# Quartered input tiles, q projections inside the norm loop, and projection blocks cut into pieces between the steps of an mLSTM scan

## The chip, the cores and the metric

One Trainium2 chip, all 8 cores of it, each with one sequence of the batch; there is no traffic between cores. The time is that of the slowest core, in device microseconds (us). Most executions agree within 0.3% (the fast ones of the kernel before lie between 3200.28 and 3208.29 us). Some fall into a second, slower state, in which the cores of one die, sometimes of both, run at a lower granted TensorE clock (0.80 to 0.96 in place of 0.97 to 0.99; the granted clock is the share of full speed that the profile records).

## The reference, cut to what matters

A decoder layer: RMS norm, one input projection, two groups of heads beside each other (dilated attention and an mLSTM), an output projection, then a gated MLP with a convolution. The change is in the norm, the mLSTM's projections and the mLSTM itself.

```python
h = _rmsnorm(x, norm_mix_g[layer]).astype(x.dtype)         # x: (8, 2048, 2048)
proj = h @ w_in[layer]
aq, ak, av, mq, mk, mv, mo, mi, mf = jnp.split(proj, IN_SPLITS, axis=-1)
...
qk = jax.nn.silu(_causal_dwconv(jnp.concatenate([mq, mk], axis=-1), ...))   # 4 taps
hm = _mlstm(mq_c, mk_c, mv, mi + b_igate, mf + b_fgate)    # 4 heads of 128, chunks of 128
hm = hm * jax.nn.sigmoid(mo)
hm = _rmsnorm(hm, mlstm_norm_g)
```

`_mlstm` goes through 16 chunks of 128 tokens in order. Each chunk computes its scores, an output from scores and carried state, and a new state for the next chunk.

## The kernel before: the parts that matter

Names used below: TensorE (PE in the profile), VectorE (DVE), ScalarE (ACT). Each engine works through its own list in program order (in the kernel before, the last matmul of a state update began at 427.07 us, but VectorE's part of the update only at 429.17, behind two operations that stand ahead of it in VectorE's list); semaphores hold an instruction until its inputs are there (VectorE stood idle until 0.10 us after ScalarE's Exp, L359, in seven tiles of eight). TensorE writes its sums into the program's eight PSUM buffers, called banks below; a bank is written again when ScalarE or VectorE has read it (TensorE waits 32.7 us in all for VectorE's reading of one in the scan of the kernel before; ScalarE's copy out of a bank is called an eviction below). "Gates" in the first stage are the mLSTM's input and forget gates; the output gate comes in the scan.

First stage: for every tile of 256 tokens, ScalarE squares all of x, TensorE sums the squares over the 2048 features with a matrix of ones, ScalarE makes 1/sqrt of it (Ln, Exp), VectorE normalises in 16 instructions, and TensorE projects v (two blocks of 16 matmuls) and the gates. The q and k projections come only after all eight tiles.

```python
def norm_a(tt):
    K.op(act, ... activation(out=sq, in_=x_t, func=AF.Square), [B_x], [B_sq])          # whole tile
    K.mm([... matmul(pb[:, 0:TA], ones, sq[:, kc, :]) for kc in range(KC)], [B_sq, B_one], [B_pb])
    ...                                                    # Ln, Exp, 16 x scalar_tensor_tensor
    if tt + 3 < NTA:
        xin(tt + 3)                                        # one 2 MB transfer into the freed tile
norm_a(0)
norm_a(1)
for tt in range(NTA):
    for tb in (2 * tt, 2 * tt + 1):
        mv_proj(tb)
    if tt + 2 < NTA:
        norm_a(tt + 2)
```

The scan: 64 dense projection blocks (16 for the output gate, 48 for the attention's v, 16 matmuls of 512 columns each) are poured between the steps of the chunks to keep TensorE busy. `next(work)` emits one whole block.

```python
for c in range(-1, NCH):
    sc_pre(c + 1)          # TensorE: scores, transposes of k, decay sums; ScalarE: Exp of the decay sums
    next(work)             # one block
    sc_out(c)              # TensorE: numerator and denominator of the output
    sc_fin(c - 1)          # TensorE: RMS sum of the chunk before; ScalarE Ln, Exp; VectorE; store
    sc_pre2(c + 1)         # VectorE: decay mask on the scores; ScalarE: scaled k
    sc_out2(c)             # ScalarE, VectorE: divide, output gate; ScalarE: Square for the RMS sum
    next(work)
    next(work)             # two blocks
    sc_upd(c, 0); sc_upd(c, 1)   # TensorE, then VectorE: new state
    if c % 2:
        next(work)         # one more after odd chunks
```

(Conditions for the first and last chunks are cut.) Scores and half of the state update share one PSUM bank, so the scores of a chunk wait until VectorE has read the update before (13 waits, 32.7 us). The decay sums and the RMS sum share another, so the RMS sum waits until ScalarE's decay Exp has read the decay sums (one wait of 0.3 us in this kernel).

The softmax here doesn't subtract the row's maximum and nothing guards it: scores larger than these inputs give would overflow.

## Time and profile before

| | us |
|---|---|
| median of 15 runs | 3206.04 |
| profiled run, slowest core (core 2) | 3205.0 |
| its first scores of the scan / first decay sums | 278.8 / 283.8 |
| its attention starts | 609.8 |
| from there to the end | 2595.2 |

Two of the waits of the first 284 us (engine and line that waited, for whom; us in total, times, longest). The line numbers are those of the kernel before:

```profile
DVE mem L361 <- ACT mem L359: 77.3, 8, 27.4
PE ps L356 <- ACT mem L355: 65.8, 8, 24.4
```

Eight waits each, one for every tile: TensorE (L356, the ones-matmuls) stands behind the Square (L355), and VectorE's normalising (L361) behind the Exp (L359). The longest of each, 24.4 and 27.4 us, is that of the first tile, while x is still landing. Together with the tile of the timeline that the prediction shows, this is a relay: one engine runs while the others stand.

### The profile page before, as it was taken

What the parts mean: (1) busy time and instruction counts of PE and PEld (TensorE: products, weight loads), DVE (VectorE), ACT (ScalarE), POOL (GpSimd) and SP (SyncE); (2) the same over time, 40 slices, a digit from 0 to 9 for tenths busy, and PEclk for the clock granted to TensorE, in tenths of its full rate; (3) what the DMA queues carried; (4) which work ended last, traced back from release to release, by engine and by line L of the source; (5) the groups of instructions that cost most, each with busy time, mean ns of one, the idle gap of its engine ahead of it and who ended that gap; (6) DMA issues with size and microseconds to landing.
All of it is one profiled execution on the core that took longest, in us unless ns stands there. A gap on an engine that the chain in (4) does not pass through costs nothing.

```text
span 3205.0 us, 43522 instructions; the slowest of 8 cores (3171.3 to 3205.0 us)
## 1 busy us (share of the span) xinstructions
PE 2929.6 (91%) x14807; PEld 1389.2 (43%) x15100; DVE 1786.4 (56%) x2452; ACT 1184.0 (37%) x1890; POOL 197.3 (6%) x347
## 2 busy tenths in 40 slices
PE   3799888999999994999899999999999978998999
PEld 2444444444444442444344444444444433443444
DVE  2465344355555551344878777777778874334333
ACT  2345544355565551111444444444444430000000
POOL 0000000000000000000111000000001100000000
PEclk8899999999999997999999999999999989999999
DMA  9232233531332309446555343334336767779784
GB/s 213 65 49 31 42 58 58 107 59 43 64 65 37 65 11 195 164 145 153 84 101 88 66 67 66 66 63 70 66 61 106 168 144 144 152 146 236 148 150 97
DMA packets 232952, 313.65 MB, mean 98 GB/s; under 512 B 24224, under 2 KB 155296, under 8 KB 230688
## 3 DMA queue, kind: packets, MB, share of 16 engines
q0 software_dynamic: 95088, 142.76, 30.8%
q1 hardware_dynamic: 137648, 168.10, 18.0%
q8 instruction: 125, 2.05, 0.3%
q14 instruction: 91, 0.75, 0.1%
HBM read 382.23 MB, written 71.30 MB: 142 GB/s over the span
## 4 chain that ended last, share of the span: by engine, by line
PE 76%; DMA 8%; DVE 8%; issue 4%; ACT 3%; DVEq 0%; another core or an unknown queue 0%; SPq 0%; ACTq 0%
PE ps L1070 43%; PE ps L709 9%; PE ps L1000 6%; PE ps L424 3%; DMA mem<-xT 3%; PE ps L508 2%; DMA mixd<-mem 2%; DMA mem<-actd 2%; PE ps L787 1%; PE ps L727 1%; DMA actd<-mem 1%; PE ps L800 1%; PE ps L372 1%; PE ps L494 1%; DVE mem L924 1%
## 5 line engine op out<-in xcount | busy, mean ns | idle before, releaser
L1070 PE MATMUL ps<-mem 128*128 128x512 bf16 x7276 | 1615.2, 381 | 77.8 <-DVE mem L924 38.9
L1070 PEld LDWEIGHTS ps<-mem 128*128 128x128 bf16 x7424 | 726.9, 98 | 965.8 <-issue 108.3
L1125 DVE SCALAR_TENSOR_TENSOR mem<-mem,cfs 128x1024 f32<-128x1024 f32 x352 | 452.0, 1284 | 225.7 <-ACT mem L1119 184.6
L709 PE MATMUL ps<-mem 128*128 128x512 bf16 x1511 | 372.3, 379 | 4.6 <-ACT mem L513 0.9
L924 DVE TENSOR_TENSOR mem<-mem 128x1024 bf16<-128x1024 bf16 (+3 forms) x324 | 305.9, 979 | 61.7 <-DMA mem<-w_down 45.0
L1091 ACT ACTIVATE mem<-ps 128x512 f32<-128x512 f32 x264 | 156.8, 594 | 424.0 <-PE ps L1070 409.8
L1253 DVE TENSOR_TENSOR mem<-ps,mem 128x512 f32<-128x512 f32 x128 | 88.3, 691 | 304.7 <-PE ps L1070 282.8
L1000 PE MATMUL ps<-mem 128*128 128x512 bf16 x1003 | 233.9, 384 | 23.2 <-DMA mem<-mixd 22.1
L1119 ACT ACTIVATE mem<-mem,cfs 128x1024 f32<-128x1024 f32 x176 | 216.9, 1233 | 11.7 <-DVE mem L1095 7.5
L709 PEld LDWEIGHTS ps<-mem 128*128 128x128 bf16 x1536 | 148.9, 98 | 162.5 <-issue 17.5
L166 POOL DMA_DIRECT2D mem<-w_up x240 | 127.4, 533 | 1237.3 <-PE ps L1070 748.7
L790 DVE TENSOR_TENSOR mem<-mem 128x512 bf16<-128x512 bf16 x216 | 88.0, 417 | 179.7 <-ACT mem L789 179.7
L720 DVE SCALAR_TENSOR_TENSOR mem<-ps,cfs,mem 128x512 bf16<-128x512 f32 x192 | 143.3, 746 | 76.7 <-ACT mem L718 66.0
L508 PE MATMUL ps<-mem 128*128 128x512 bf16 x749 | 175.6, 389 | 1.6 <-issue 0.4
L1095 DVE TENSOR_TENSOR mem<-ps,mem 128x512 f32<-128x512 f32 x264 | 172.9, 683 | 1.3 <-PE ps L1070 1.2
L1000 PEld LDWEIGHTS ps<-mem 128*128 128x128 bf16 x1024 | 101.1, 99 | 146.1 <-issue 27.9
L789 ACT ACTIVATE mem<-ps 128x512 bf16<-128x512 f32 x216 | 126.7, 589 | 88.5 <-PE ps L787 87.0
L1012 DVE TENSOR_TENSOR mem<-ps,mem 128x512 f32<-128x512 f32 x64 | 44.3, 692 | 177.3 <-PE ps L1020 107.6
L1017 ACT ACTIVATE mem<-mem 128x512 bf16<-128x512 f32 x64 | 40.2, 629 | 239.9 <-DVE mem L1012 239.9
L508 PEld LDWEIGHTS ps<-mem 128*128 128x128 bf16 x768 | 77.0, 101 | 90.2 <-issue 8.6
L361 DVE SCALAR_TENSOR_TENSOR mem<-mem,cfs 128x256 bf16<-128x256 f32 x128 | 62.0, 484 | 90.7 <-ACT mem L359 77.3
L424 PE MATMUL ps<-mem 128*128 128x512 bf16 x501 | 111.6, 383 | 0.8 <-issue 0.2
(118 smaller groups left out, 2321.9 us busy)
## 6 DMA issues: line engine op xcount, KB each, us to landing
mem<-w_up POOLq DMA_DIRECT2D x240, 256.0 KB, 5.0
mem<-w_down POOLq DMA_DIRECT2D x60, 640.0 KB, 8.2
actd<-mem SPq DMA_DIRECT2D x88, 256.0 KB, 3.9
mem<-actd SPq DMA_DIRECT2D x16, 1280.0 KB, 17.2
mem<-xT SPq DMA_DIRECT2D x8, 2048.0 KB, 20.5
mem<-xT SPq DMA_DIRECT2D x64, 256.0 KB, 3.3
x1d<-mem SPq DMA_DIRECT2D x64, 256.0 KB, 3.7
mem<-x1d SPq DMA_DIRECT2D x64, 256.0 KB, 5.2
```

The source lines that it names most:

```text
L166: eng.e.dma_start(out=o_, in_=i_).then_inc(sb.dsem, 16)
L424: bk, B_bk = dense(5, [lambda e, b, kc=kc: e.matmul(b[:], sl[:, kc, hm * 128:(hm + 1) * 128], hT[:, kc, tsl], start=(kc == 0), stop=(kc == ...
L508: bk, B_bk = dense(3, [lambda e, b, kc=kc: e.matmul(b[:], hT[:, kc, c0:c0 + 128], sl[:, kc, :], start=(kc == 0), stop=(kc == KC - 1)) for ...
L709: ins = pe.e.matmul(bank[:], sl[:, kc, c0:c0 + 128], hT[:, kc, tsl], start=(kc == 0), stop=(kc == KC - 1))
L720: K.op(dve, lambda e: e.scalar_tensor_tensor(out=sc[nm], in0=bank[:], scalar=cf[:, gcol:gcol + 1], in1=tab[:, tsl], op0=ALU.mult, op1=ALU. ...
L924: K.op(dve, lambda e: e.tensor_tensor(out=out, in0=a, in1=b, op=op), [B_a, B_b], [B_out])
L1000: K.mm([lambda e, kc=kc: e.matmul(ps[bi][:], wo_v[jb][:, kc, (jc % 4) * 128:(jc % 4 + 1) * 128], mixT[:, T, kc, :], start=(kc == 0), stop= ...
L1070: K.mm([lambda e, l=l, r=r, s_=(first and i == 0): e.matmul(ps[bi][:], l, r, start=s_, stop=False, skip_group_check=True) for i, (l, r) in ...
L1091: K.op(act, lambda e: e.activation(out=snap[si], in_=ps[bank][:], func=AF.Copy), [B_ps[bank]], [B_snap[si]])
L1095: K.op(dve, lambda e: e.tensor_tensor(out=y, in0=ps[bank][:], in1=snap[si], op=ALU.add), [B_ps[bank], B_snap[si]], [self.B_y[gv]])
L1119: K.op(act, lambda e: e.activation(out=self.a[gv], in_=self.y[gv][:, 2:1026], func=AF.Identity, scale=self.wc(gv, 2), bias=cf[:, CF_FCB + ...
L1125: K.op(dve, lambda e, k=k: e.scalar_tensor_tensor(out=self.a[gv], in0=self.y[gv][:, k:k + 1024], scalar=self.wc(gv, k), in1=self.a[gv], op ...
```

## The change

Its intent: in the first stage, fill TensorE's pauses with q projection blocks, and square x ahead of its use; in the scan, take the dense block out from between the scores and the output, and spread the filler evenly.

```diff
@@ first stage @@
+    # x tile moved to make room: the third one lies over the space of the constants cb
     def xin(tt):
-        K.dma(sp, xs[tt % 3], xT_v[:, :, tt * TA:(tt + 1) * TA], B_xs[tt % 3], True)
+        for q in range(4):
+            K.dma(sp, xs[tt % 3][:, 4 * q:4 * q + 4, :], ..., B_xs[tt % 3][q], True)
...
-    K.dma(pool, cb[:], cbd, B_cb, True)          # now behind the q projections
+    def norm_sq(tt): ...                         # four Squares, one for each quarter
+    def norm_h(tt): ...                          # ones-matmuls by quarters, Ln, Exp, normalise
...
+    norm_sq(0); norm_h(0); norm_sq(1); norm_h(1)
+    mv_proj(0); norm_sq(2); mv_proj(1); norm_h(2)
+    for tt in range(2, NTA):
+        if tt + 1 < NTA:
+            norm_sq(tt + 1)
+        mq_proj(2 * tt - 4)
+        if tt + 1 < NTA:
+            mq_proj(2 * tt - 3)
+            norm_h(tt + 1)
+        mv_proj(tt)
+    for i in range(11, 16):
+        mq_proj(i)
...                                              # gate constants moved behind this point
@@ scan @@
+        def block(lr, reads):                    # a dense block that yields after every 4 matmuls
...
-            sc_pre(c + 1)
-        next(work)
+            sc_pre(c + 1)
+        if c < 0:
+            some(4)
...
             sc_out2(c)
-        next(work)
-        next(work)
+        some(8)                                  # 8 pieces = two blocks
+        if ok(c):
+            sc_sq(c)                             # the Square that ended sc_out2
...
             sc_upd(c, 1)
-        if c % 2:
-            next(work)
+        some(6)                                  # one and a half blocks
```

The number of matmuls is the same.

More of the change, by code (lines that the diff above doesn't have):

```diff
@@ L296, in build @@
     xs, B_xs = [], []
-    for i, o in enumerate((0, 16384, 49152)):
-        v, B = alloc(A0 + o, KC * TA, F32, "xs%d" % i)
-        xs.append(v.rearrange("p (k t) -> p k t", t=TA))
-        B_xs.append(B)
-    o = A0 + 65536
-    gt, B_gt = alloc(o, 128, F32, "gt")
-    e1, B_e1 = alloc(o + 512, 64, F32, "e1")
-    lf, B_lf = alloc(o + 768, 64, F32, "lf")
-    ib, B_ib = alloc(o + 1024, 64, F32, "ib")
-    ebias, B_eb = alloc(o + 1280, 64, F32, "ebias")
-    gt, e1, lf, ib, ebias = [a.rearrange("p (c g) -> p c g", c=16) for a in (gt, e1, lf, ib, ebias)]
-    OT = o + 1792
+    for i, o in enumerate((A0 + 16384, A0 + 49152, 160768)):
+        v = mview(o, KC * TA, F32).rearrange("p (k t) -> p k t", t=TA)
+        xs.append(v)
+        B_xs.append([K.mbuf("xs%d_%d" % (i, q), o + q * 4096, o + (q + 1) * 4096) for q in range(4)])
+    OG = A0 + 65536
+    OT = OG + 1792
     o = OT
-    sqA, B_sqA, rsA, B_rsA = [], [], [], []
+    sqA, B_sqA = [], []
     for i in range(2):
-        v, B = alloc(o, KC * TA, BF16, "sqA%d" % i)
-        sqA.append(v.rearrange("p (k t) -> p k t", t=TA))
-        B_sqA.append(B)
+        sqA.append(mview(o, KC * TA, BF16).rearrange("p (k t) -> p k t", t=TA))
+        B_sqA.append([K.mbuf("sqA%d_%d" % (i, q), o + q * 2048, o + (q + 1) * 2048) for q in range(4)])
         o += 8192
-        v, B = alloc(o, TA, F32, "rsA%d" % i)
-        rsA.append(v)
-        B_rsA.append(B)
-        o += 1024
+    rsA, B_rsA = zip(*[alloc((OG, o)[i], TA, F32, "rsA%d" % i) for i in range(2)])
+    o += 1024
     acc, B_acc, xp, B_xp = [], [], [], []
@@ L332, in build @@
     tl, B_tl = alloc(o, 32, F32, "tl")
+    assert o + 128 <= 160768
     tl = tl.rearrange("p (j w) -> p j w", w=4)
@@ L340, in xin, with by_tile @@
     def xin(tt):
-        K.dma(sp, xs[tt % 3], xT_v[:, :, tt * TA:(tt + 1) * TA], B_xs[tt % 3], True)
+        for q in range(4):
+            K.dma(sp, xs[tt % 3][:, 4 * q:4 * q + 4, :], xT_v[:, 4 * q:4 * q + 4, tt * TA:(tt + 1) * TA], B_xs[tt % 3][q], True)
+    def by_tile(b, lo, hi):
+        bl = [K.buf(b.name) for _ in range(NT)]
+        for b_ in bl:
+            K.inherit(b_, [b])
+            K.regions.append((lo, hi, b_))
+        return bl
     xin(0)
@@ L349, in build, with norm_sq, norm_h @@
     w_issue()
-    K.dma(pool, cb[:], cbd, B_cb, True)
-    def norm_a(tt):
-        x_t, B_x, sq, B_sq, r, B_r = xs[tt % 3], B_xs[tt % 3], sqA[tt % 2], B_sqA[tt % 2], rsA[tt % 2], B_rsA[tt % 2]
+    def norm_sq(tt):
+        x_t, sq = xs[tt % 3], sqA[tt % 2]
+        for q in range(4):
+            qs = slice(4 * q, 4 * q + 4)
+            K.op(act, lambda e: e.activation(out=sq[:, qs, :], in_=x_t[:, qs, :], func=AF.Square),
+                 [B_xs[tt % 3][q]], [B_sqA[tt % 2][q]])
+    def norm_h(tt):
+        x_t, sq, r, B_r = xs[tt % 3], sqA[tt % 2], rsA[tt % 2], B_rsA[tt % 2]
         pb, B_pb = ps[6 + tt % 2], B_ps[6 + tt % 2]
-        K.op(act, lambda e: e.activation(out=sq, in_=x_t, func=AF.Square), [B_x], [B_sq])
-        K.mm([lambda e, kc=kc: e.matmul(pb[:, 0:TA], ones, sq[:, kc, :], start=(kc == 0), stop=(kc == KC - 1))
-              for kc in range(KC)], [B_sq, B_one], [B_pb])
+        for q in range(4):
+            K.mm([lambda e, kc=kc: e.matmul(pb[:, 0:TA], ones, sq[:, kc, :], start=(kc == 0), stop=(kc == KC - 1))
+                  for kc in range(4 * q, 4 * q + 4)], [B_sqA[tt % 2][q], B_one], [B_pb])
         K.op(act, lambda e: e.activation(out=r, in_=pb[:, 0:TA], func=AF.Ln, scale=1.0 / D, bias=EPS), [B_pb], [B_r])
@@ L362, in norm_a @@
                 out=hT[:, kc, tt * TA:(tt + 1) * TA], in0=x_t[:, kc, :], scalar=cf[:, CF_G1 + kc:CF_G1 + kc + 1],
-                in1=r, op0=ALU.mult, op1=ALU.mult), [B_x, B_r, B_cf], [B_hT[tt]])
+                in1=r, op0=ALU.mult, op1=ALU.mult), [B_xs[tt % 3][kc // 4], B_r, B_cf], [B_hT[tt]])
         if tt + 3 < NTA:
             xin(tt + 3)
-    slot, B_slot = w_next()
-    sl = wv(slot)
-    def mv_proj(tb):
-        c0 = tb * 128
-        bk, B_bk = dense(5, [lambda e, b, kc=kc: e.matmul(b[:], hT[:, kc, c0:c0 + 128], sl[:, kc, :], start=(kc == 0),
-                                                          stop=(kc == KC - 1)) for kc in range(KC)],
-                         [B_slot, B_hT[tb // 2]])
-        K.op(act, lambda e: e.activation(out=mvt[:, tb, :], in_=bk[:], func=AF.Copy), [B_bk], [B_mv])
-        K.mm([lambda e, kc=kc: e.matmul(ps[5][:, tb * 8:(tb + 1) * 8], hT[:, kc, c0:c0 + 128], wg[:, kc, :],
-                                        start=(kc == 0), stop=(kc == KC - 1)) for kc in range(KC)],
-             [B_hT[tb // 2], B_wg], [B_ps[5]])
@@ L380, in build, with mv_proj @@
-    norm_a(0)
-    norm_a(1)
-    for tt in range(NTA):
-        for tb in (2 * tt, 2 * tt + 1):
-            mv_proj(tb)
-        if tt + 2 < NTA:
-            norm_a(tt + 2)
-    w_issue()
+    w_mv, B_wmv = w_next()
+    w_mq, B_wmq = w_next()
+    w_mv, w_mq = wv(w_mv), wv(w_mq)
+    def mv_proj(tt):
+        for tb in (2 * tt, 2 * tt + 1):
+            c0 = tb * 128
+            bk, B_bk = dense(5, [lambda e, b, kc=kc: e.matmul(b[:], hT[:, kc, c0:c0 + 128], w_mv[:, kc, :],
+                                                              start=(kc == 0), stop=(kc == KC - 1)) for kc in range(KC)],
+                             [B_wmv, B_hT[tt]])
+            K.op(act, lambda e: e.activation(out=mvt[:, tb, :], in_=bk[:], func=AF.Copy), [B_bk], [B_mv])
+            K.mm([lambda e, kc=kc: e.matmul(ps[5][:, tb * 8:(tb + 1) * 8], hT[:, kc, c0:c0 + 128], wg[:, kc, :],
+                                            start=(kc == 0), stop=(kc == KC - 1)) for kc in range(KC)],
+                 [B_hT[tt], B_wg], [B_ps[5]])
@@ new lines, in build, with conv_proj @@
+    pend_silu = []
+    def conv_proj(part, sl, B_slot, dstT, B_d, tt, hm):
+        tsl = slice(tt * TT, (tt + 1) * TT)
+        bk, B_bk = dense(5, [lambda e, b, kc=kc: e.matmul(b[:], sl[:, kc, hm * 128:(hm + 1) * 128], hT[:, kc, tsl],
+                                                          start=(kc == 0), stop=(kc == KC - 1))
+                             for kc in range(KC)], [B_slot] + hTt(tt))
+        j = part * 4 + hm
+        wc = lambda k: cf[:, CF_MCW + j * 4 + k:CF_MCW + j * 4 + k + 1]
+        xi = rot["xp"]
+        rot["xp"] += 1
+        x_, B_x, a_, B_a = xp[xi % 3], B_xp[xi % 3], acc[xi % 2], B_acc[xi % 2]
+        K.op(act, lambda e: e.activation(out=x_[:, 3:3 + TT], in_=bk[:], func=AF.Copy), [B_bk], [B_x])
+        K.op(act, lambda e: e.activation(out=a_, in_=bk[:], func=AF.Identity, scale=wc(3),
+                                         bias=cf[:, CF_MCB + j:CF_MCB + j + 1]), [B_bk, B_cf], [B_a])
+        while pend_silu:
+            pend_silu.pop(0)()
+        K.op(dve, lambda e: e.tensor_copy(out=x_[:, 0:3], in_=tl[:, j, 0:3]), [B_tl[j]], [B_x])
+        for k in (2, 1, 0):
+            K.op(dve, lambda e, k=k: e.scalar_tensor_tensor(out=a_, in0=x_[:, k:k + TT], scalar=wc(k), in1=a_,
+                                                            op0=ALU.mult, op1=ALU.add), [B_x, B_cf, B_a], [B_a])
+        K.op(dve, lambda e: e.tensor_copy(out=tl[:, j, 0:3], in_=x_[:, TT:TT + 3]), [B_x], [B_tl[j]])
+        pend_silu.append(lambda: K.op(act, lambda e: e.activation(out=dstT[:, hm, tsl], in_=a_, func=AF.Silu),
+                                      [B_a], [B_d[tt]]))
@@ new lines, in build @@
+    mqT, B_mq = alloc(A0, 4 * S, BF16, "mqT")
+    mqT = mqT.rearrange("p (h t) -> p h t", t=S)
+    B_mq = by_tile(B_mq, A0, A0 + 16384)
+    mq_proj = lambda i: conv_proj(0, w_mq, B_wmq, mqT, B_mq, i // 4, i % 4)
+    norm_sq(0)
+    norm_h(0)
+    norm_sq(1)
+    norm_h(1)
+    mv_proj(0)
+    norm_sq(2)
+    mv_proj(1)
+    norm_h(2)
+    for tt in range(2, NTA):
[6 more added lines that the diff above has]
+        mv_proj(tt)
@@ new lines, in build @@
+    w_issue()
+    for i in range(11, 16):
+        mq_proj(i)
+    w_issue()
+    while pend_silu:
+        pend_silu.pop(0)()
+    K.dma(pool, cb[:], cbd, B_cb, True)
+    gt, B_gt = alloc(OG, 128, F32, "gt")
+    e1, B_e1 = alloc(OG + 512, 64, F32, "e1")
+    lf, B_lf = alloc(OG + 768, 64, F32, "lf")
+    ib, B_ib = alloc(OG + 1024, 64, F32, "ib")
+    ebias, B_eb = alloc(OG + 1280, 64, F32, "ebias")
+    gt, e1, lf, ib, ebias = [a.rearrange("p (c g) -> p c g", c=16) for a in (gt, e1, lf, ib, ebias)]
@@ L402, in gates_2 @@
         K.op(act, lambda e: e.activation(out=ebias, in_=ib, func=AF.Exp), [B_ib], [B_eb])
-    mqT, B_mq = alloc(A0, 4 * S, BF16, "mqT")
     mkT, B_mk = alloc(A0 + 16384, 4 * S, BF16, "mkT")
     sgo, B_sgo = alloc(A0 + 49152, 4 * S, BF16, "sgo")
-    mqT, mkT, sgo = [a.rearrange("p (h t) -> p h t", t=S) for a in (mqT, mkT, sgo)]
-    def by_tile(b, lo, hi):
-        bl = [K.buf(b.name) for _ in range(NT)]
-        for b_ in bl:
-            K.inherit(b_, [b])
-            K.regions.append((lo, hi, b_))
-        return bl
@@ L415, in build @@
-    B_mq, B_mk = by_tile(B_mq, A0, A0 + 16384), by_tile(B_mk, A0 + 16384, A0 + 32768)
-    pend_silu = []
-    for part in range(2):
-        slot, B_slot = w_next()
-        sl = wv(slot)
-        dstT, B_d = (mqT, B_mq) if part == 0 else (mkT, B_mk)
-        for tt in range(NT):
-            tsl = slice(tt * TT, (tt + 1) * TT)
-            for hm in range(NHM):
-                bk, B_bk = dense(5, [lambda e, b, kc=kc: e.matmul(b[:], sl[:, kc, hm * 128:(hm + 1) * 128], hT[:, kc, tsl],
-                                                                  start=(kc == 0), stop=(kc == KC - 1))
-                                     for kc in range(KC)], [B_slot] + hTt(tt))
-                if part == 0 and tt == 0 and hm == 0:
-                    gates_2()
-                j = part * 4 + hm
-                wc = lambda k: cf[:, CF_MCW + j * 4 + k:CF_MCW + j * 4 + k + 1]
-                xi = rot["xp"]
-                rot["xp"] += 1
-                x_, B_x, a_, B_a = xp[xi % 3], B_xp[xi % 3], acc[xi % 2], B_acc[xi % 2]
-                K.op(act, lambda e: e.activation(out=x_[:, 3:3 + TT], in_=bk[:], func=AF.Copy), [B_bk], [B_x])
-                K.op(act, lambda e: e.activation(out=a_, in_=bk[:], func=AF.Identity, scale=wc(3),
-                                                 bias=cf[:, CF_MCB + j:CF_MCB + j + 1]), [B_bk, B_cf], [B_a])
-                while pend_silu:
-                    pend_silu.pop(0)()
-                K.op(dve, lambda e: e.tensor_copy(out=x_[:, 0:3], in_=tl[:, j, 0:3]), [B_tl[j]], [B_x])
-                for k in (2, 1, 0):
-                    K.op(dve, lambda e, k=k: e.scalar_tensor_tensor(out=a_, in0=x_[:, k:k + TT], scalar=wc(k), in1=a_,
-                                                                    op0=ALU.mult, op1=ALU.add), [B_x, B_cf, B_a], [B_a])
-                K.op(dve, lambda e: e.tensor_copy(out=tl[:, j, 0:3], in_=x_[:, TT:TT + 3]), [B_x], [B_tl[j]])
-                pend_silu.append(lambda d=dstT[:, hm, tsl], a_=a_, B_a=B_a, B_d=B_d[tt]: K.op(
-                    act, lambda e: e.activation(out=d, in_=a_, func=AF.Silu), [B_a], [B_d]))
-        w_issue()
@@ L447, in build @@
+    mkT, sgo = [a.rearrange("p (h t) -> p h t", t=S) for a in (mkT, sgo)]
+    B_mk = by_tile(B_mk, A0 + 16384, A0 + 32768)
+    slot, B_slot = w_next()
+    sl = wv(slot)
+    for i in range(16):
+        conv_proj(1, sl, B_slot, mkT, B_mk, i // 4, i % 4)
+        if i == 0:
+            gates_2()
+    w_issue()
     pend_silu.pop(0)()
@@ L488, in dense_work @@
     def dense_work():
+        def block(lr, reads):
+            bi = rot["mm"] % 3
+            rot["mm"] += 1
+            K.deps(pe, reads, [B_ps[bi]])
+            for kc in range(KC):
+                ins = pe.e.matmul(ps[bi][:], *lr(kc), start=(kc == 0), stop=(kc == KC - 1))
+                if kc % 4 == 3 and kc < KC - 1:
+                    yield
+            K.mark(pe.sig(ins), reads, [B_ps[bi]])
+            blk[:] = ps[bi], B_ps[bi]
+        blk = [None, None]
         slot, B_slot = w_next()
@@ L493, in dense_work @@
             for hm in range(NHM):
-                bk, B_bk = dense(3, [lambda e, b, kc=kc: e.matmul(b[:], sl[:, kc, hm * 128:(hm + 1) * 128], hT[:, kc, tsl],
-                                                                  start=(kc == 0), stop=(kc == KC - 1))
-                                     for kc in range(KC)], [B_slot] + hTt(tt))
+                yield from block(lambda kc: (sl[:, kc, hm * 128:(hm + 1) * 128], hT[:, kc, tsl]), [B_slot] + hTt(tt))
+                bk, B_bk = blk
                 K.op(act, lambda e: e.activation(out=sgt, in_=bk[:], func=AF.Exp, scale=-1.0), [B_bk], [B_sgt])
@@ L507, in dense_work @@
                 c0 = tb * 128
-                bk, B_bk = dense(3, [lambda e, b, kc=kc: e.matmul(b[:], hT[:, kc, c0:c0 + 128], sl[:, kc, :],
-                                                                  start=(kc == 0), stop=(kc == KC - 1))
-                                     for kc in range(KC)], [B_slot, B_hT[tb // 2]])
+                yield from block(lambda kc: (hT[:, kc, c0:c0 + 128], sl[:, kc, :]), [B_slot, B_hT[tb // 2]])
+                bk, B_bk = blk
                 v_, B_v = vst[rot["vs"] % 3], B_vst[rot["vs"] % 3]
@@ L571, in sc_out2, with sc_sq @@
         K.op(dve, lambda e: e.tensor_tensor(out=hg, in0=hg, in1=sgo[:, :, csl], op=ALU.mult), [B_hg, B_sgo], [B_hg])
+    def sc_sq(c):
+        hg, B_hg = hg2[c % 2], B_hg2[c % 2]
         K.op(act, lambda e: e.activation(out=sqh, in_=f4(hg), func=AF.Square), [B_hg], [B_sqh])
@@ L622, in build, with some @@
     work = dense_work()
+    def some(n):
+        for _ in range(n):
+            next(work)
     ok = lambda c: 0 <= c < NCH
@@ L642, in build @@
             sc_upd(c, 1)
-        if c % 2:
-            next(work)
-    next(work)
+        some(6)
     sc_fin(NCH - 1)
@@ L1567, in run @@
     for b in range(ncores):
-        in_maps.append({"xT": np.ascontiguousarray(inp["x"][b].T), "w_in": w_in, "w_out": w_out, "w_up": w_up,
+        in_maps.append({"xT": np.ascontiguousarray(inp["x"][b].T),
+                        "w_in": w_in, "w_out": w_out, "w_up": w_up,
                         "w_down": w_down, "cb": cbn, "cf": cfn, "cs": cs})
```

## The prediction, made before the changed kernel ran

> **What bounds the kernel now.** I read the page first, then the busy time by stage, then the timeline of the first 170 us, then the chain of waits inside the mLSTM scan. Stage limits come from where the first instruction of each line falls: norm and mLSTM v projection 0 to 163 us, q and k projections with their convolution to 284, scan to 610, then attention, output projection and ConvFFN. Busy time by stage (start and end, length; PE, weight loads, DVE, ACT, POOL; granted clock; DMA share; GB/s):
>
> ```profile
> 0.00:284.00 284.00, 208.83 (x1174) 106.18 (x1194) 144.43 (x294) 108.33 (x141) 9.61 (x14) 0.90 0.47 94
> 284.00:610.00 326.00, 285.95 (x1621) 154.26 (x1654) 123.76 (x234) 158.83 (x285) 4.91 (x5) 0.93 0.31 58
> 610.00:1238.00 628.00, 581.40 (x3672) 294.53 (x3742) 336.73 (x551) 351.75 (x600) 15.65 (x14) 0.98 0.34 62
> 1500.00:3205.00 1705.00, 1619.20 (x7294) 728.57 (x7441) 1095.29 (x1256) 522.70 (x797) 160.76 (x303) 0.99 0.57 110
> ```
>
> The change touches only the first two rows. In both, PE is idle some of the time and its clock is below full; nothing after 610 us is edited, so what those two stages lose or gain should arrive at the end unchanged. One tile of the first stage, on the timeline:
>
> ```profile
> 88.72 3.61 ACT L355 ACTIVATE mem<-mem 128x4096 bf16<-128x4096 f32 x1
> 92.47 3.32 PE L356 MATMUL ps<-mem,ones 128*128 128x256 bf16 x16 [4.02 <-ACT mem L355]
> 96.42 0.42 ACT L359 ACTIVATE mem<-mem 128x256 f32<-128x256 f32 x1
> 96.93 9.31 DVE L361 SCALAR_TENSOR_TENSOR mem<-mem,cfs 128x256 bf16<-128x256 f32 x16 [6.79 <-ACT mem L359]
> 99.48 3.61 PE L372 MATMUL ps<-mem 128*128 128x512 bf16 x16
> 104.05 3.61 ACT L355 ACTIVATE mem<-mem 128x4096 bf16<-128x4096 f32 x1
> ```
>
> Square (3.61 us) runs alone, PE waits 4.02 us for it, then sums the squares at half speed (3.32 us for 16 matmuls of 256 columns). A tile takes 15.3 us here (88.72 to 104.05), of which real projection work is about 7.7. In the scan, this is one lap of the chain of waits (start, length, what), cut:
>
> ```profile
> 413.82 0.38 PE ps L522 x4
> 415.38 3.45 PE ps L508 x16
> 420.04 0.61 ACT mem L603
> 421.46 0.70 DVE mem L606
> 427.77 0.70 DVE mem L570
> 429.17 0.49 DVE mem L592
> 431.35 0.59 PE ps L522 x4
> ```
>
> It is a loop: scores of the next chunk (L522), a dense projection block of 3.45 us (L508), the outputs, the RMS sums, ACT, then DVE's in-order list from L606 to the state update L592, which frees the score bank for the next L522. So the lap lasts 17.53 us, and the dense block in it is on the path, not filler. The waits of PE in the scan say the same:
>
> ```profile
> PE ps L522 <- DVE mem L592: 32.7, 13, 5.2
> ```
>
> [...] after the idle gaps of the norm, weight loads stand 0.43 us apart, later a block of 16 takes 3.45 us, 0.216 each. [...] the granted clock is 1.00 from 180 to 230 us with PE busy 49.74 of 50 us. [...] L592, whose matmuls ended at 427.1, waits for L571 ahead of it. [...] The trace shows 1.28 us and the Silu starting right after (176.98, 178.27), so I use 1.28. [...] while the weights stream beside them, x tiles take about 18 us each (19.2, 38.0, then 72.3 landed), with the DMA share at 1.0 until 80 us.
>
> **The change, part by part.** First, x comes in quarters, each with its own Square and its own four ones-matmuls. On tiles 0 and 1 only the last quarter remains behind the landing: 0.95 us instead of 3.62, and 0.9 instead of 3.5. x tile 1 landed at 38.0, so the first v block starts near 40.0 instead of 45.2. Saves 5.
>
> Second, Square is issued a tile ahead and mq blocks are put into the norm loop. PE work of a full iteration, at full clock: two mq blocks 6.9, ones-matmuls [...] 1.7, two v blocks with gates 7.7 (3.86 each): 16.3 us. Does another engine exceed that? DVE: normalise 9.31 plus two convolutions of 2.9 = 15.1. ACT: Square 3.8, four conv copies 2.8, two Silus 1.25, Ln and Exp 0.8, two evictions 1.2, and two table loads 2.6, because Silu and Ln/Exp now alternate: 12.5. (That is about 12 more loads, 15 us of ACT, hidden if PE is the bound.) The latency from the ones-matmuls to a finished hT is 3.1 + 9.3 = 12.4 us, against 16.3 until the v blocks want it. So 16.3 stands.
>
> The clock of this stage then reads: first v blocks 40.0; the second pair needs hT of tile 1, 50.7, and ends at 58.5; ones-matmuls of tile 2 to 60.3; the first mq block needs the second weight slot, which landed 58.5 us after its issue at 5.8, so 64.3: a new wait of 4 us; tile 3 of x lands near 70 and the iteration ends at 80.7. Four full iterations: 145.9. Last: one mq and two v blocks, 11.2: 157.1. Then five mq blocks, 17.3: 174.4. The k weights can start only when the v blocks are done, and the same load took 19.0 us before: they land at 176.5 to 177, a new wait of 2.5. Then k blocks 55.2, gate cumsum 3.7 and about 1: scan at 237 instead of 284. Saves 47 (the 5 above included). The constant load moved behind it is not wanted until the scan.
>
> Third, the scan. Taking the dense block out from between scores and outputs shortens the lap from 17.53 to 14.1 us. PE's own work per chunk is 3.5 blocks x 3.45 = 12.1, plus scores, transposes and decay sums 1.56, outputs 0.9, RMS sum 0.2, update 0.45: 15.2. PE so becomes the bound with a margin of 1 us[...]. I take 15.6 for small waits. Before, ten laps from 376.14 to 564.90 took 18.88 each: 3.28 saved on eleven laps is 36. The first four laps also carry the output gate, three ACT passes a block: ACT needs some 14 us of 15, and stands ahead of the decay Exp, so I take 17.5 against 18.5, saving 4. The last waits save 2. Sum 42. Square moved behind the dense blocks only frees ACT, which was idle 26.9 us there; PE had not waited for it.
>
> Sum: 47 + 42 = 89. 3206 - 89 = 3117 us, 2.8% less.
>
> **Rivals.** (a) The norm loop turns DVE- or ACT-bound: DVE has 15.1 of 16.3 us, and each semaphore hop costs it 0.1. For it: convolution and normalise alternate behind table loads. Against: hT has 3.9 us of slack. If an iteration takes 18.5, 2.2 x 5 = 11 us go: 3128. (b) Weights arrive too late for the compressed stage: both waits above (4 and 2.5) grow if the x quarters take more of the DMA. Against: dropping the constants from the early queue leaves more. Worth up to 12: 3129. (c) The scan stays latency-bound: the margin is 1 us, and Cbf, the decay Exp and the evictions share one ACT queue. If a lap takes 17 instead of 15.6, 15 us go: 3132. (d) The gain is given back later, at the attention start or by a lower clock. Against: attention, at 97% busy PE, is fed by the same sequence of prefetches, and the clock holds 1.00 in dense stages. If half the gain went: 3161. [...]
>
> **Range and chances.** (a), (b) and (c) are each likely in part and would add up to about 3150 only together; the upside is some 15 us. I predict 3117, with 3096 to 3145 holding it 8 times in 10. Over 2% faster means under 3142: 0.87. Within 2%: 0.12. Slower by over 2%: 0.01, since no instruction is added on the path but hidden table loads.
>
> **What would show it.** The first gate cumsum decay matmul of the scan (L527 before) should start near 237 instead of 283.8: later than 245 means (a) or (b), and the waits of PE tell which, DVE's normalise or the weight DMA. Attention should start 89 us earlier, near 521, and the time from there to the end should stay 2595. Laps of the scan should be 15 to 16 us with PE's wait for L592 gone from its list; if a wait for ACT's decay Exp or for Cbf stands there instead, it is (c). The granted clock should rise to about 0.97 in both stages. About 16 table loads should appear where 4 were. A span after attention longer than before would show (d), and my premise that the stages add up would be wrong.

The 1.28 us at 176.98 is a table load, ScalarE's ACT_TABLE_LOAD, in front of the first Silu. Of the 16 matmuls of 256 columns on that timeline (from 92.47), most start 0.213 us apart, at a granted clock of 0.50 (92.1 to 95.3 us); the last two stand 0.110 us apart.

## The result, and the profile after

| | before | after |
|---|---|---|
| median of all runs, us | 3206.04 (15 runs) | 3123.06 (11 runs) |
| ratio | | 0.9742, 95% interval 0.9733 to 0.9752 |
| first scores, mean of 8 cores | 278.1 | 241.5 |
| attention starts, mean of 8 cores | 608.7 | 531.2 |
| end, mean of 8 cores | 3187.8 | 3109.6 |
| TensorE clock, mean of the slowest core | 0.968 | 0.980 |

The ratio is the mean time of one kernel's fast runs over that of the other's fast runs of the same rounds, so it is not quite the ratio of the two medians. The change makes the kernel 2.6% faster, 83 us by the medians; 89 were predicted. By the means of the cores of the two profiled runs it is 78.

The rows by core come from one profiled run each: the time from a core's first instruction to the first one of a line. Two profiled runs of the very same kernel (the second is told below) differ by 1.6 us in the first scores, by 1.3 in the length of the scan and by 3.7 in what comes after, always as means of the cores; the cores of one run spread by 20 to 31 us in what comes after. Differences below that say nothing. So the stages read: first stage 36.6 us shorter, scan 40.9 shorter (330.6 to 289.7), the rest unchanged (2579.1 and 2578.4).

Line numbers of the two kernels, for reading what follows:

| | before | after |
|---|---|---|
| Square of x, ones-matmuls, normalise | L355, L356, L361 | L356, L363, L368 |
| v blocks; q and k blocks | L372; L424 | L381; L393 |
| gate log; gate cumsum on TensorE | L394; L397 | L453; L456 |
| scores; decay sums; decay Exp | L522; L527; L529 | L559; L564; L566 |
| dense blocks of the scan | L494, L508 | L522 |
| state update on VectorE; RMS sum | L592; L602 | L632; L642 |

Busy time by stage on the slowest core after the change (its columns as in the prediction's first fence; the stages are cut at its own first scores, attention and ConvFFN):

```profile
0.00:240.80 240.80, 199.16 (x1162) 100.63 (x1184) 138.92 (x286) 124.25 (x173) 8.45 (x13) 0.98 0.55 110
240.80:532.60 291.80, 273.73 (x1630) 146.56 (x1660) 128.01 (x243) 160.74 (x288) 6.22 (x6) 0.98 0.35 65
532.60:1118.90 586.30, 568.19 (x3570) 286.08 (x3641) 327.29 (x534) 340.44 (x581) 12.20 (x11) 1.00 0.29 54
1421.40:3121.00 1699.60, 1616.85 (x7279) 726.79 (x7425) 1093.69 (x1254) 521.88 (x796) 160.21 (x303) 0.99 0.57 109
```

The clock rose from 0.90 and 0.93 to 0.98 in both stages, and in the scan TensorE is busy 94% of the time (273.73 of 291.80) where it was 88% (285.95 of 326.00), while its busy time itself fell by 12 us: the same matmuls at a higher clock (the median of the decay sums' matmuls went from 328 to 275 ns).

One iteration of the norm loop, on the timeline after:

```profile
95.86 6.85 PE L393 MATMUL ps<-mem 128*128 128x512 bf16 x31
96.05 3.88 ACT L356 ACTIVATE mem<-mem 128x1024 bf16<-128x1024 f32 x4
...
102.55 1.91 PE L363 MATMUL ps<-mem,ones 128*128 128x256 bf16 x16
...
104.29 3.62 PE L381 MATMUL ps<-mem 128*128 128x512 bf16 x15
...
105.13 1.28 ACT L365 ACT_TABLE_LOAD   x1
...
107.42 9.32 DVE L368 SCALAR_TENSOR_TENSOR mem<-mem,cfs 128x256 bf16<-128x256 f32 x16 [0.18 <-ACT mem L366]
...
112.22 6.85 PE L393 MATMUL ps<-mem 128*128 128x512 bf16 x31
```

Read the PE lines: two q blocks, the ones-matmuls in 1.91 us, 0.109 apart (3.32 before), two v blocks, and the next q blocks at 112.22. None of these lines carries a wait in brackets. The Square of the next tile (96.05) now lies under the q blocks. The iteration takes 16.36 us and holds two more blocks than a 15.3 us tile did before.

A steady lap of the scan, in the chain of waits after, with `...` for the outputs and the state update's 0.06 us pieces:

```profile
377.02 0.22 PE ps L559 x4
...
377.46 0.95 PE ps L564 x8
...
379.30 0.32 PE ps L642
...
380.76 5.78 PE ps L522 x26
...
390.27 1.89 PE ps L522 x8
392.16 0.22 PE ps L559 x4
```

Before, this chain ran through ScalarE and VectorE; now every piece of it is PE's own. The lap is 15.14 us long (377.02 to 392.16), where 17.5 and 20.1 alternated. What TensorE still waits for in the scan:

```profile
PE ps L642 <- ACT mem L566: 10.4, 5, 3.4
PE ps L564 <- DVE mem L558: 4.4, 1, 4.4
```

The 32.7 us of waits for the state update are gone. The 4.4 us wait at the scan's start was there before. The first line is new in this size (one wait of 0.3 us before): it is the RMS sum that waits for the decay Exp, the sign that the prediction gave for its rival (c).

One more new wait stands between the stages. TensorE, and one ScalarE line, at the first k block:

```profile
176.31 3.61 PE L393 MATMUL ps<-mem 128*128 128x512 bf16 x16 [1.46 <-DMA mem<-w_in]
...
179.94 1.28 ACT L451 ACT_TABLE_LOAD   x1
182.39 5.57 PE L456 MATMUL ps<-mem,cfs 128*128 128x4 f32 x32 [2.47 <-DVE mem L453]
...
188.20 53.01 PE L393 MATMUL ps<-mem 128*128 128x512 bf16 x235 [0.24 <-issue]
```

The k weights come 1.46 us late, and the gate cumsum then waits 2.47 us for the gates' log, and runs slower after it (5.57 us; 3.63 before). The first k matmuls behind it are slow, too: their weight loads stand 0.43 us apart from 188.20 to 190.76, where 0.22 is usual.

### The profile page after: what moved, and what is told of

It is laid out like the page before. It is cut to its first block, busy times and chain, and to the rows that moved or that the text cites. A ratio compares the mean times of both kernels' runs of the same rounds, so it can differ in the third digit from the quotient of the medians.

```text
span 3121.2 us, 43707 instructions; the slowest of 8 cores (3093.6 to 3121.2 us)
## 1 busy us (share of the span) xinstructions
PE 2908.4 (93%) x14805; PEld 1376.0 (44%) x15100; DVE 1784.8 (57%) x2452; ACT 1201.4 (38%) x1926; POOL 196.9 (6%) x347
## 4 chain that ended last, share of the span: by engine, by line
PE 79%; DMA 7%; DVE 6%; issue 4%; ACT 3%; SPq 1%; DVEq 0%; another core or an unknown queue 0%; ACTq 0%; POOLq 0%; POOL 0%
PE ps L1114 44%; PE ps L753 10%; PE ps L1044 6%; PE ps L522 6%; PE ps L393 3%; DMA mixd<-mem 2%; DMA actd<-mem 2%; PE ps L831 1%; PE ps L771 1%; PE ps L381 1%; DMA mem<-actd 1%; PE ps L844 1%; PE ps L772 1%; DVE mem L1215 1%; DVE mem L968 1%
## 5 line engine op out<-in xcount | busy, mean ns | idle before, releaser
L1114 PE MATMUL ps<-mem 128*128 128x512 bf16 x7276 | 1616.4, 381 | 78.7 <-DVE mem L968 40.1
L1114 PEld LDWEIGHTS ps<-mem 128*128 128x128 bf16 x7424 | 726.7, 98 | 968.0 <-issue 111.0
L753 PE MATMUL ps<-mem 128*128 128x512 bf16 x1500 | 371.9, 379 | 4.6 <-ACT mem L550 0.9
L1044 PE MATMUL ps<-mem 128*128 128x512 bf16 x1004 | 233.9, 384 | 22.1 <-DMA mem<-mixd 21.1
L522 PE MATMUL ps<-mem 128*128 128x512 bf16 x994 | 229.6, 385 | 2.2 <-issue 0.8
L753 PEld LDWEIGHTS ps<-mem 128*128 128x128 bf16 x1536 | 148.9, 98 | 162.6 <-issue 17.6
L1044 PEld LDWEIGHTS ps<-mem 128*128 128x128 bf16 x1024 | 101.1, 99 | 145.1 <-issue 27.1
L522 PEld LDWEIGHTS ps<-mem 128*128 128x128 bf16 x1024 | 100.9, 99 | 119.3 <-issue 7.3
L393 PE MATMUL ps<-mem 128*128 128x512 bf16 x499 | 112.9, 385 | 5.4 <-DMA mem<-w_in 4.3
L1215 DVE TENSOR_TENSOR mem<-mem 128x1024 bf16<-128x1024 f32 x88 | 106.8, 1213 | 4.3 <-DMA actd<-mem 4.1
```

The source lines that it names most:

```text
L393: bk, B_bk = dense(5, [lambda e, b, kc=kc: e.matmul(b[:], sl[:, kc, hm * 128:(hm + 1) * 128], hT[:, kc, tsl], start=(kc == 0), stop=(kc == ...
L522: ins = pe.e.matmul(ps[bi][:], *lr(kc), start=(kc == 0), stop=(kc == KC - 1))
L753: ins = pe.e.matmul(bank[:], sl[:, kc, c0:c0 + 128], hT[:, kc, tsl], start=(kc == 0), stop=(kc == KC - 1))
L1044: K.mm([lambda e, kc=kc: e.matmul(ps[bi][:], wo_v[jb][:, kc, (jc % 4) * 128:(jc % 4 + 1) * 128], mixT[:, T, kc, :], start=(kc == 0), stop= ...
L1114: K.mm([lambda e, l=l, r=r, s_=(first and i == 0): e.matmul(ps[bi][:], l, r, start=s_, stop=False, skip_group_check=True) for i, (l, r) in ...
L1215: K.op(dve, lambda e: e.tensor_tensor(out=ao[i], in0=self.a[0], in1=self.a[1], op=ALU.mult), [self.B_a[0], self.B_a[1]], [B_ao[i]])
```

## The experiments

All use the changed kernel ("after") as the base, except where told. Times are of fast runs; "scan" is from the first scores to the start of attention, mean of the cores, and 289.7 us in the changed kernel.

### The two stages apart

The old scan behind the new first stage, and the new scan behind the old first stage:

```diff
 # stage only: after, with dense_work, sc_out2 and the chunk loop of the kernel before
 # scan only:  the kernel before, with dense_work, sc_out2/sc_sq and the chunk loop of after
```

> The changed first stage (norm, v, q and k projections) with the old scan. If the two parts simply add: the first scores of the scan start about 37 us earlier than before (241.5 against 278.1 us, mean of the cores), the scan lasts as long as before (331 us) and the whole comes to about 3206 - 37 = 3169 us. Rival, the gain of one part depends on the other (for instance weights for the scan that now come too late, or the clock): the scan is then longer than 335 us and the time above 3175.

> The changed scan behind the old first stage. If the parts add: scores start at 278 us as before, the scan lasts 290 us instead of 331, the whole about 3206 - 41 = 3165 us. Rival as in the run beside it: a time above 3172 or a scan above 295 us would say that part of its gain came from the first stage.

Measured: stage only 3161.1 us (only one of its four runs was fast, so there is no interval), first scores at 240.6, scan 328.0. Scan only 3157.9 to 3160.5 us, ratio 0.9859 (0.9837 to 0.9882), first scores at 278.3, scan 287.4. The kernel before took 3203 to 3206 beside them. So each part gives its gain without the other, 43 and 45 us by the means of the fast runs, and the sum of 88 is near the 83 of both; the 5 us between are about the scatter of such sums. The expectations were 8 us too high for the stage (3169) and 6 for the scan (3165).

### The dense block put back into the lap

The one part undone that the prediction calls the cause in the scan:

```diff
-        if c < 0:
-            some(4)
+        some(4)
...
-        some(6)
+        some(6 if c < 0 else 2)
```

> The changed kernel with one change undone: a whole dense block (four pieces) stands again between the scores and the outputs of every chunk, and four pieces fewer behind the state update; the split of blocks into pieces, 3.5 blocks per chunk, the moved Square and the first stage stay. Theory, the block was on the lap of waits: a lap goes from 15.1 back to about 14.1 + 3.45 = 17.5 us, PE waits for the state update of DVE again, and the whole is some 11 to 15 laps x 2.4 = 26 to 36 us longer than the changed kernel: 3149 to 3159. Rival, the gain came from spreading the filler evenly[...]: laps stay under 16 us and the time within 8 us of 3123.

Measured: 3154.5 to 3158.9 us, ratio 0.9851 (0.9829 to 0.9874), scan 321.1. That is 34 us slower than the changed kernel, and the scan accounts for 31 of them. TensorE's list of waits has its old entry back:

```profile
PE ps L559 <- DVE mem L632: 32.6, 13, 3.2
```

13 waits and 32.6 us, against 13 waits and 32.7 us in the kernel before. The fine split, the even 3.5 blocks and the moved Square were all still in this kernel. So the place of the block is worth 31 of the scan's 41 us, because the block stands on the lap's chain of waits, and the rival, that even filling brings the whole gain, falls. It does not bring the old laps back in full: over the last ten they average 18.1 us here on the slowest core, 18.9 in the kernel before and 15.9 in the changed one, and the 20.1 us laps have become 17.5 to 19.2. The other 10 us belong to the rest of the scan's edit (split, even spread, Square) together; with the block on the lap no run takes these apart.

### Whole blocks in place of pieces

```diff
-        some(6)
+        some(4 if c < 0 or c % 2 == 0 else 8)
```

> The changed kernel with whole dense blocks only: behind the state update one block after even chunks and two after odd ones, in place of one and a half each. Theory: with three blocks TensorE has only 10.35 + 3.1 = 13.5 us of work in a lap that the chain of waits holds at 14.1 or more, so half of the laps gain a wait of 0.6 to 1 us and the others none: the scan is 4 to 8 us longer (294 to 298) and the time near 3129. Rival, the split is without effect: within 2 us of the run beside it[...].

Measured, beside a repeat of the changed kernel on the same chip:

> The changed kernel unaltered, run again beside the next three on the same chip, so that differences of some us can be read: about 3123 us, first scores at 241 us, scan 290 us.

The repeat took 3123.9 to 3128.8 us (ratio 0.9754, scan 288.4), whole blocks 3122.0 to 3128.2 (ratio 0.9751, scan 288.7): no difference. My expectation was wrong in its sum, though its mechanism showed. On the slowest core six new waits for the state update came, 4.0 us together, as worked out for laps with three blocks; two waits for ScalarE's bf16 copy of the state (2.7 us) came too, but the waits for ScalarE's decay Exp fell from some 8 to 11 us per core in the repeat to 4.1 to 4.6 (3.2 of dense blocks and 1.4 of RMS sums on that core). One paid for the other. The laps say the same: the later ones alternate between 14.18 and 16.87 us, 15.5 in the mean, where the changed kernel has 15.14, but two laps of 19.1 us that it has (explained below) are gone. So an even lap is worth 0.4 us, and in the whole scan cutting blocks in half is worth nothing here.

### The moved Square

```diff
     def sc_out2(c):
         ...
+        K.op(act, ... activation(out=sqh, in_=f4(hg), func=AF.Square), [B_hg], [B_sqh])
...
-        if ok(c):
-            sc_sq(c)
```

> The changed kernel with the Square of the RMS sums put back before the dense blocks, where it stood. Theory: TensorE did not wait for ScalarE there and still has margin, the scan stays at 290 +- 2 us and the time at 3123 +- 4. Rival, the move mattered: ScalarE stands waiting for the DVE product while blocks want eviction, laps grow by 0.5 us or more and the scan by 8.

Measured: 3138.2 to 3140.7 us, ratio 0.9802 (0.9774 to 0.9831), 17 us more than the changed kernel; scan 302.3: 12.6 us longer. The rival of this run holds, and a sentence of my prediction falls. From the timeline of this run:

```profile
384.23 0.63 ACT L609 ACTIVATE mem<-mem 128x512 bf16<-128x512 f32 x1 [1.69 <-DVE mem L608]
384.77 1.07 ACT L550 ACTIVATE mem<-ps 128x512 bf16<-128x512 f32 x2
385.49 3.61 PE L522 MATMUL ps<-mem 128*128 128x512 bf16 x16 [1.59 <-ACT mem L550]
```

ScalarE stands 1.69 us in front of the Square (L609) until VectorE's product is there, and the evictions of two finished blocks (L550) stand behind it in its list. TensorE runs out of free PSUM banks and waits 1.59 us. In this run's list of waits that is 9.7 us in 7 waits on most cores. The kernel before had the same Square in the same place, and its list of waits shows none for an eviction in the laps, but 32.7 us in 13 waits for the state update. That this slack hid the Square is argued: no run moves the Square alone in the old scan. As the laps stand after the change, an order in ScalarE's list that showed no wait before shows one.

### Whole tiles of x

```diff
-        for q in range(4):
-            K.dma(sp, xs[tt % 3][:, 4 * q:4 * q + 4, :], ..., B_xs[tt % 3][q], True)
+        K.dma(sp, xs[tt % 3], xT_v[:, :, tt * TA:(tt + 1) * TA], B_xs[tt % 3][0], True, extra_writes=...)
 # and one Square for the tile
```

> The changed kernel with x loaded and squared in whole tiles again (one transfer of 2 MB, one Square of 3.6 us). Theory, the quarters shorten only what lies behind a landing on the first two tiles: the first v block starts some 5 us later (about 43 instead of 38 us) and, as later tiles are bound by TensorE, nothing is added after that; some of the 5 us vanish in the wait for the q weights: 3124 to 3128 us. Rival, the whole Square blocks ScalarE in every iteration and delays the convolutions: an iteration goes from 16.4 to over 17 us, and the time to over 3132.

Measured: 3125.5 to 3136.8 us, ratio 0.9773 (0.973 to 0.9816), first scores at 246.7, 5.2 us later. The first v block started at 43.3 us (37.8 with quarters), and the iterations stayed at 16.36 us (84.14 to 100.50 on the timeline). So the quarters are worth about 5 us, once, at the start, as the theory has it. On the way, on the slowest core, the delay was 5.4 us at the first v block, 7.0 at the ones-matmuls of the third tile (63.70 against 56.71) and 4.0 at the first q block (65.44 against 61.44), where the 2.83 us wait for the q weights was gone: part of it did vanish there, as I had remarked. A new wait of 1.96 us for a convolution followed, and 4.6 were left at 84.14. The 8.7 us by the mean of the fast runs (3131.1 against 3122.4) includes a scatter of this kernel's runs of over 10 us; I read the value from the stage.

### The gate cumsum later

The new wait between the stages, taken away by giving the gates' log more time:

```diff
-        if i == 0:
+        if i == 3:
             gates_2()
```

> The changed kernel with the gate cumsum issued on TensorE after the fourth k block instead of after the first. Theory: the 2.5 us wait of TensorE for the gates' log (Exp, Ln and negation, behind the last q convolutions) and about 2 us of half-speed matmuls after it vanish, so the scan's first scores come 4 to 5 us earlier (237 us as a mean of the cores, 241.5 before), the time about 3118.5. Rival: the wait only moves (to the scan, which needs the gate bias), and the time stays within 1.5 us of 3123.

Measured: 3113.0 and 3121.8 us, ratio 0.9733 (0.9695 to 0.9772); first scores at 235.0, 6.5 us earlier than in the changed kernel and 4.9 earlier than in its repeat; scan 286.8. No wait for L453 is left in TensorE's list. By the stage mark the 4 to 5 us are there; by the time, two runs 9 us apart leave it open.

### Silu out of the norm loop

```diff
-        ... activation(out=dstT[:, hm, tsl], in_=a_, func=AF.Silu)
+        ... activation(out=dstT[:, hm, tsl], in_=a_, func=AF.Copy if part == 0 else AF.Silu)
```

> The changed kernel with Copy in place of Silu for the q convolutions, so the result is wrong on purpose; it takes away about 11 of the 16 table loads (1.28 us each, 14 us of ScalarE). Theory, they are hidden behind TensorE: only the load before the gates' Exp and the 1.4 us wait of the last iteration gain, first scores 1 to 3 us earlier than 241.5. Rival, the switching costs the stage: 8 us or more earlier.

The changed kernel has 16 table loads, most of them these two groups (line, engine, operation, count; busy us, ns of one; idle before):

```profile
L411 ACT ACT_TABLE_LOAD x7 | 9.0, 1283 | 0.4 <-DVE mem L410 0.3
L365 ACT ACT_TABLE_LOAD x5 | 6.4, 1283 | 0.1
```

With Copy 4 loads are left in all. Measured: 3121.5 to 3122.9 us, ratio 0.9749 (0.9727 to 0.9771): the time is that of the changed kernel. First scores at 236.9, 4.6 us earlier (3.0 earlier than in the repeat): the wait for the gates' log is down to 0 to 1.9 us on the eight cores, from 2.5 to 4.1, since the table load before it (179.94 on the timeline above) was a link to the log. That is at or above the 1 to 3 expected, and somewhat less than moving the cumsum gave. The time did not follow, because the rest of this run was some 6 us longer (2584.9 after the start of attention), within the scatter. So the twelve additional loads, 15 us of ScalarE, are mostly hidden; what shows is 3 to 5 us, and the wait that shrank with them is the one behind the load before the gates.

### ScalarE in the first laps

TensorE's new wait for the decay Exp, 10.4 us: two tries to relieve ScalarE in the laps that carry the output gate. First its three passes (Exp, Ln, Exp) issued a piece later; then gate blocks alternating with v blocks after the first six, with the gate tracked by time tile.

```diff
 # later:
                 bk, B_bk = blk
+                yield
                 ... three activations
-                yield
 # alternating:
+        for i in range(6):
+            yield from gate_block(i)
+        # then v_block(0), gate_block(6), v_block(1), gate_block(7), ...
```

> The changed kernel with the three ScalarE passes of an output-gate block issued one piece later, that is behind the decay Exp of the next chunk where a block ends a lap. Theory: in the first laps the RMS-sum matmul of TensorE waits 10.4 us in 5 waits for that Exp, because the passes stand ahead of it; this wait falls under 3 us and the scan goes from 290 to 281 to 284 us. Rival, ScalarE is simply full in these laps: another wait takes its place and the scan stays above 287.

> The changed kernel with only the alternation of output-gate and v blocks after the first six (and the gate tracked by time tile). Theory, ScalarE's queue is too full in the first laps (three passes for every block, standing ahead of the decay Exp): with half the gate blocks per lap the wait of TensorE for that Exp falls from 10 us to under 3 and the scan from 290 to 281 to 283 us. Rival, the waits only spread over twice the laps: scan above 287.

Measured: later, 3121.6 and 3124.9 us, ratio 0.9752 (0.9723 to 0.978), scan 286.7; alternating, 3116.1 to 3124.0, ratio 0.9732 (0.9715 to 0.9748), scan 284.6. The scan is 2 to 3 us shorter with the first, hardly more than the 1.3 between two runs of one kernel, and 4 to 5 with the second, both less than expected; the wait for the decay Exp fell to 6.8 and 6.3 us on the slowest cores, not under 3. The timeline of the changed kernel shows why. Only three of its five waits, 5.9 us (1.17, 1.30 and 3.43), lie in the gate's laps. The other two look like this:

```profile
391.20 1.15 POOL L166 DMA_DIRECT2D mem<-w_in  x1 [67.00 <-remote]
...
403.05 8.54 SPq L166 DMA_DIRECT2D vd<-mem  x4
...
410.59 0.60 ACT L550 ACTIVATE mem<-ps 128x512 bf16<-128x512 f32 x1 [2.92 <-DMA vd<-mem]
411.09 0.59 ACT L566 ACTIVATE mem<-ps 128x512 f32<-128x512 f32 x1
...
411.82 0.38 PE L642 MATMUL ps<-mem,ones 128*128 128x512 bf16 x1 [2.24 <-ACT mem L566]
```

A weight load starts at 391.20. While it runs, the store of a v block takes 7.5 us (403.05 to 410.59) instead of the usual 1.7 (median of the 36 stores issued from 332 to 490 us), the three staging buffers of v are all in flight, ScalarE stands 2.92 us at the eviction L550 until one is free, and behind it the decay Exp L566, and TensorE for it. The same happens at 476 us. Each of these two laps is 4.0 us longer than the others: 2.2 us are the wait, and after it some matmuls run slower (from 411 to 427 us the dense blocks' matmuls take 417 ns in the mean and up to 634, where 379 is usual). With alternating blocks the gate's share fell from 5.9 to 1.9 us (0.54, 0.58, 0.16, 0.65), and 4.4 us of the other kind stayed (1.23 and 3.15). So ScalarE's queue in the gate's laps is one cause, shown by the alternation; that the rest hangs on the v stores is what the waits say, and no run with a fourth staging buffer was made.

### A version with three mends

The cumsum after the fourth k block, alternating gate and v blocks, and the scan's first dense block ahead of the first chunk's scores, in place of the 4.4 us wait:

```diff
-        if ok(c + 1):
-            sc_pre(c + 1)
         if c < 0:
             some(4)
+        if ok(c + 1):
+            sc_pre(c + 1)
 # with the two edits above
```

> The changed kernel with three mends together: the gate cumsum behind the fourth k block (4 to 6 us, as seen alone), the first dense block of the scan ahead of the first chunk's scores and decay sums (takes the place of the 4.4 us wait of TensorE for the end of the k convolutions: 4 us), and output-gate blocks alternating with v blocks after the first six, with the gate tracked by time tile (8 us if the wait for the decay Exp goes). Sum 16 to 18: about 3106 us, first scores not comparable as a block stands ahead of them, attention starting at 514 instead of 531 us (mean of the cores). Rival, part of it turns into new waits for ScalarE or for the v weights: above 3112.

Measured: 3106.3 to 3113.4 us, median of the fast runs 3107.8, correct, ratio 0.9699 (0.9684 to 0.9715). That is 17 us less than the repeat of the changed kernel beside it (3108.9 against 3126.3, means of the fast runs), and attention starts at 512.4 against 528.3. It is the best version here.

## Why the prediction was right, and which of its terms were off

The time, 3123 us, lies 6 us above the predicted 3117 and inside the range. The stage marks are less close: attention starts 77.5 us earlier as a mean of the cores, not 89; that the medians show 83 and not 78 lies within the scatter of what comes after. By its steps:

- **The norm loop becomes TensorE-bound at 16.3 us an iteration.** Right: 16.36, four times in a row. The landing times drove the start as said: the first v block at 37.8 (predicted 40.0), the wait for the q weights 2.83 us until 61.44 (4 us until 64.3 predicted), the loop's last v blocks done at 157.4 (157.1). Of the stage's 36.6 us the run with whole tiles shows 5 to be the quarters'; that the rest comes from the q blocks in the loop and the Square a tile ahead is read from the timelines, and no run undoes one of them, or the later load of the constants, alone. Rival (a) did not come true: VectorE is busy 9.3 + 5.7 us of the 16.36 and nobody waits for it there, but for 2 us at the second tile and 1.4 in the last iteration.
- **The k weights come late.** Right: 1.46 us on that core, 2.5 predicted.
- **"Scan at 237 instead of 284. Saves 47."** This is the term that failed, twice. 237 was worked out as the end of the k blocks, where the first scores stand; 284 is the first decay sum, 5 us later in the kernel before. Like with like, 278.8 to 237 is 42. The sign to watch was skewed in the same way: the first decay sum came at 246.1, past the 245 that was to mean (a) or (b), and meant neither, for the 4.4 us wait in front of it was there before. And the sum gave the gate cumsum 3.7 us, as it had before, without asking for its inputs: the change moved the gates' log from well ahead of it to just ahead. It waited 2.5 us on that core (2.5 to 4.1 on the eight) and then took 5.57 us for 3.63. Moving the cumsum took the wait away and brought the first scores 5 to 6.5 us forward. Measured for the stage: 36.6 as a mean of the cores, 42 less this wait.
- **The lap of the scan.** Right, and shown: the block put back gives the old waits and 31 of the 41 us. The sum said 15.2 us of TensorE's own work; the lap came to 15.14. The allowance up to 15.6 was not needed in steady laps, and was used up elsewhere: two laps are 4 us longer, behind the late v stores, which no rival had named. Rival (c) came true in its sign and not in its size: TensorE does wait for the decay Exp, 10.4 us in all, but the lap is not 17. In sum 40.9 against 42, and that this is so close is partly luck: on the slowest cores the last ten laps gave 30 us (189.0 to 159.4) where 3.28 each, 33, was allowed, and the gate's four laps gave 8 (18.5 to 16.5 each) where 4 was.
- **"Square moved behind the dense blocks only frees ACT."** Wrong. The prediction took it from waits measured at the old lap, with slack; with that edit alone undone the scan is 12.6 us longer. The sum was not hurt because the edit was there.
- **Table loads.** 16 predicted, 16 seen, 1283 ns each with the next instruction right behind (load at 105.13 for 1.28 us, the Ln that needs it at 106.42), and hidden but for 3 to 5 us, as the run with Copy shows.
- **What comes after stays.** Right: 2579.1 and 2578.4 us as means of the cores, and from 532.6 to 1118.9 us the granted clock is 1.00 with TensorE busy 568.19 of 586.30 us, so rival (d) falls.
- **Readings that say less than they seem to.** The x tiles landing at 19.2, 38.0 and 72.3 (the third of these is the fourth tile) show at most that x and the weights share the DMA engines (share 1.02 from 0 to 80 us). And (a), (b) and (c) together are 11 + 12 + 15 = 38 us, which is 3155 and not "about 3150".

## What to carry to other kernels

When a dependent loop and filler work share an engine, find the lap in the chain of waits and ask of every filler block whether it stands on the lap or beside it; here the same blocks, a few lines further down, were worth 31 us of scan. Waits measured under one bound did not hold under the next: after the bound moved to TensorE, the Square's old place in ScalarE's list, which had shown no wait, cost 12.6 us of scan; such orders have to be asked again. When work is moved, follow the inputs of what it now stands in front of, too: the gate cumsum did not move, but the work that hid its inputs did. And compare stage marks of the same instruction, not of two neighbours.
